# Holding late weight copies behind their step, freeing the gate transposes and moving embedding products in a two-layer decoder trunk

## The chip, the cores and the metric

The kernel runs on one core of a Trainium2 chip. The metric is the device time of one execution in microseconds (us), as a median over runs. A core has a matrix engine (PE, with its weight loads shown as PEld), a vector engine (DVE), a scalar engine (ACT), a general engine (POOL) and a queue engine that issues most of the DMA transfers (SP). Each works through its own list of instructions in order, and they wait for one another through semaphores. The order of each list is fixed when the program is built.

## The reference

The input is x, 512 tokens of 1024 features. Two layers follow one another; each is a mixer, a gated MLP with a causal convolution of width 3, and an input embedding that is gated and added:

```python
for i in range(2):
    h = h + (ab_mixer if i == 0 else nsa_mixer)(rms_norm(h), ...)
    h = h + conv_ffn(rms_norm(h), w_up[i], conv_w[i], conv_b[i], w_down[i])
    e = rms_norm(p[i] @ ple_w[i])                  # 512 x 256 by 256 x 1024
    h = h + sigmoid(rms_norm(h) @ ple_w_gate[i]) * e
```

The change touches the second mixer, `nsa_mixer`, alone. It has 16 query heads of 64 in two groups, and three branches for each head: attention over compressed blocks of keys (`kc`, `vc`), over selected blocks, and over a window. With 512 tokens the selection takes every block and the window covers everything before a query, so both of these are causal attentions over all earlier keys, with keys and values of their own. The three results of a head are weighted by `gates = sigmoid(h @ w_gate + b)`, 48 columns, and summed; then comes an output projection `o @ w_out`.

## The kernel before

All activations lie with features on the 128 partitions, in eight blocks of 128 features by 512 tokens. Products are made in a split form: each operand is cut into a high part (rounded to the fp32r format) and a low part (what is left), and `mm3` (lines 204 to 207) issues three matmuls, high by high, high by low and low by high. A weight of 128 x 1024 is therefore loaded by a DMA on SP into a buffer `wr` (4 of them), copied by ACT into a high part `wh` (3 buffers), and subtracted on DVE or POOL into a low part `wl` (3 buffers). `load_late` (line 169) does this in three separate steps: it issues the DMA, with a raised priority, and gives back two functions, one for the high part on ACT and one for the low part on POOL. Both stand on line 175, which is how the profile names them.

A scheduler orders what the Python code traces. It goes by priority, which is the order of the trace unless a block raises it, and lets an instruction go ahead of earlier ones when its inputs and buffers are there by its own estimate. `self.behind(engine)` limits that: the instructions traced inside it are placed on that engine after the last instruction that had been traced for it up to then.

The mixer begins with projections. `thin()` makes the 48 gate values as rows, `sg` (its last step is the sigmoid on line 823), and `gate_columns(sg)` turns them into columns: four PE transposes (line 829) into a PSUM bank, a DVE copy (line 830) and a small DVE multiplication. These stand among the products of the first query half (`q0`, lines 205 to 207) and of the small network that compresses keys (`hidden_step`, lines 903 to 906). In the kernel before, the call comes after the third `hidden_step` and is held behind it on PE.

The attention itself is a list of 96 steps, six for each head, made by `UNITS`: query blocks 3, 3, 2, 2, 1 and 0, the larger ones with one branch at a time and the smaller ones with both. A step makes scores on PE (lines 1096 and 1097), the masked maximum on DVE (1099), the exponential and its sum on ACT (1101), and the scaling by the gate on POOL (1112). Four steps later (`LAG`) the same unit is transposed on PE (1127), copied as a high part on ACT (1130), given its low part on DVE (1389), and after two more steps multiplied with the values on PE (1152). A head's result is copied out by ACT (1159, 1162), put together by SP's DMAs (1165 to 1168) and added and split on POOL (1182 to 1184).

Between these, other jobs are put into the steps by a planner written in the kernel. `load` holds an estimate in ns for each engine ("T" is PE, "V" DVE, "S" ACT, "G" POOL) and step; `then(step, jobs)` puts a job into the first step from `step` on in which no engine falls behind by more than `SLACK`, at `PACE` = 1950 ns a step; and a job of a step is traced at its end. The jobs that matter here are these.

- `embed(m, s0)`: block m of the embedding product of layer 1, two `mm3` (six matmuls), then a copy out of PSUM on ACT (line 1692; for the first steps on DVE) and a DMA on SP that stores it (line 1693). `EMBED_AT[m]` is its first step. It is called for m below `emb.done` = `KD - LEFT` = 7; the eighth block is made at the start of the MLP instead. `EMBED_AT[4]` is also the step for which the second half of the embedding's weight is loaded.
- `out_first(m, s0)`: half of block m of the output projection, four `mm3`, from step `OUT_AT[m]` = 63, 67, 72, 78, 86, 99, 101, 103 on.
- `late(step, src, use)`: a weight by `load_late`. The DMA is traced eight steps ahead of `step`, the high part from six ahead, the low part a step later. It is used for the embedding's second weight (step 12), four weights of the output projection's first half (for steps 63, 72, 86 and 101) and two of its second half (steps 100 and 102). With the planner's own numbers the six high parts of the output projection's weights fall on steps 57, 66, 80, 95, 96 and 97. In the kernel before, a low part of a weight used after step 40 is held behind POOL's last traced instruction, and a high part is not held.

Of the kernel before, what the change touches and what calls it, by code (L numbers as in the profile page):

```python
# [34 lines left out]
Q1_AT = 0  # L35
LAST_AT = (100, 102)
PACE, SLACK = 1950, {"T": 2500, "V": 1000, "S": 1000, "G": 1500}
EMBED_AT = (0, 1, 2, 6, 12, 17, 22, 27)
OUT_AT = (63, 67, 72, 78, 86, 99, 101, 103)
UNITS = ((3, (0,)), (3, (1,)), (2, (0,)), (2, (1,)), (1, (0, 1)), (0, (0, 1)))  # L40
BANKS = {"a": 4, "b": 3, "o": 1}
# [25 lines left out]
class Trunk:  # L67
# [706 lines left out]
    def nsa_mixer(self):  # L774
        nc, I, tc = self.nc, self.I, self.tc
# [3 lines left out]
        with ExitStack() as ctx:  # L779
# [28 lines left out]
            def thin():  # L808
                self.cycle = ("b",)
                ps = [self.ws(I["w_cmp"][w], n) for w in range(2)]  # L810
                self.norm_scale(n)
                hT = []
                for w in range(2):
                    t = self.sc()
                    nc.vector.tensor_tensor(t, ps[w], n.b, ALU.mult)
                    hT.append(t)
                w, ps = self.packed(I["w_ngate"]), self.ps("o")
                self.cycle = ("a",)
                for k in range(KD):
                    self.packed_step(ps, w, n, k)  # L820
                sg = self.packed_sum(ps)
                nc.vector.tensor_tensor(sg[0:48], sg[0:48], n.b[0:48], ALU.mult)
                nc.scalar.activation(sg[0:48], sg[0:48], AF.Sigmoid, bias=self.col(C_NGB, 0, 48))
                return hT, sg

            def gate_columns(sg):
                pt = self.ps("b")
                for j in range(NTT):
                    nc.tensor.transpose(pt[:, 48 * j : 48 * j + 48], sg[0:48, j * P : (j + 1) * P], self.ident[0:48, 0:48])
                nc.vector.tensor_copy(gate.rearrange("p a b c -> p (a b c)"), pt[:, 0 : 48 * NTT])  # L830
                nc.vector.tensor_scalar(gate[:, 0, :, 0], gate[:, 0, :, 0], valid, None, ALU.mult)
# [64 lines left out]
            def hidden_step(which, xs, ph, c):  # L896
                hi, lo = self.load(I["w1"][which, c])
                for q in range(4):
                    jj = 4 * c + q
                    ws = slice(256 * q, 256 * q + 256)  # L900
                    x = xs[c // 2][:, jj % 8]
                    if jj:
                        nc.tensor.matmul(ph[0:64, 0:256], x[:, 0], lo[:, ws], start=False, stop=False)
                    nc.tensor.matmul(ph[:, 0:256], x.rearrange("p a s -> p (a s)"), hi[:, ws], start=jj == 0, stop=jj == 15)
                    if jj == 0:
                        nc.tensor.matmul(ph[0:64, 0:256], x[:, 0], lo[:, ws], start=False, stop=False)
# [285 lines left out]
            hT, sg = thin()  # L1192
# [9 lines left out]
            xv = blocks(1, hT[1])  # L1202
            q0 = self.Tokens(self, I["w_q"][0], n)
            q0.steps(0, 1)
            hidden_step(0, xk, ph, 2)
            with self.behind(nc.tensor):
                gate_columns(sg)
            q0.steps(1, 2)
            hidden_step(0, xk, ph, 3)
            hk = hidden(ph)  # L1210
# [69 lines left out]
            def fits(e, step, n):  # L1280
                late = 0
                for k in range(step + 12):
                    late = max(0, late + load[e][k] + n * (k == step) - PACE)
                    if k >= step and late > SLACK[e]:
                        return False
                return True

            def then(step, *jobs):
                for e, n, f in jobs:
                    if f is None:  # L1290
                        step += n
                        continue
                    while not fits(e, step, n):
                        step += 1
                    load[e][step] += n
                    todo[step].append(f)
                    step += 1
                return step

            def stack(sts, hd, s0):  # L1300
                got = []
                copy = "VS"[hd % 2 == 0], 620, lambda: q_stack_copy(hd, got[0])
                last = then(s0, ("T", 440, lambda: got.append(q_stack_t(sts, hd, "b" if s0 < LAG else "a"))), copy)
                assert last <= 6 * hd, ("stack", hd, last)
                return last

            def comp_first(c, s0):
                got = {}
                x = lambda name, *a: lambda: getattr(got["x"], name)(*a)
                last = then(s0, ("T", 530, lambda: (got.update(x=Compressed(c, "a")), got["x"].products(0))))  # L1310
                then(last, ("V", 840, x("masked", 0)))
                last = then(last, ("T", 530, x("products", 1)), ("V", 840, x("masked", 1)))
                last = comp_last(got, last, ("V", 680, x("maxima")), ("G", 1050, x("shift")), ("", 1, None))
                assert last <= 24 * c + LAG + VALUES_LAG + 2, (c, last)
# [6 lines left out]
            def late(step, src, use):  # L1321
                got = []

                def low():
                    with self.behind(nc.gpsimd) if step > 40 else ExitStack():
                        got[2]()

                todo[max(step - 8, 0)].append(lambda: got.extend(self.load_late(src)))
                then(max(step - 6, 2), ("S", 1060, lambda: got[1]()), ("G", 1500, low))
                todo[step].append(lambda: use(got[0]))  # L1330

            def embed(m, s0):
                got = []
                then(s0, ("T", 1360, lambda: got.append(emb.products(m, ew[m // 4], "b" if s0 < LAG else "a"))), ("V" if s0 < LAG else "S", 650, lambda: emb.keep(m, got[0], s0 < LAG)))

            def out_first(m, s0):
                got = []
                then(s0, ("T", 2720, lambda: got.append(self.out_products(wo[m // 2], m, *outs[0]))), ("V", 690, lambda: self.out_add(m, got[0])))
# [17 lines left out]
            comp_first(2, max(stack(sts1, 8 + i, ready_at + 1 + i) for i in range(4)))  # L1356
            comp_first(3, max(stack(sts1, 12 + i, 52 + 2 * i) for i in range(4)) + 1)
            late(EMBED_AT[4], I["w_ple"][1, 1], lambda w: ew.append(w))
            for i in range(4):
                late(OUT_AT[2 * i], I["w_nso"][0, i], lambda w, i=i: wo.update({i: w}))  # L1360
            for i in range(2):
                late(LAST_AT[i], I["w_nso"][1, i], lambda w, i=i: wo.update({4 + i: w}))
            for m in range(KD):
                if m < emb.done:
                    embed(m, EMBED_AT[m])
                out_first(m, OUT_AT[m])
# [494 lines left out]
```

## Time and profile before

| | |
|---|---|
| median of 3 runs | 1321.82 us (1321.33 to 1322.67) |
| the profiled execution | 1321.43 us, of which the span from first to last instruction is 1319.7 us |
| PE busy | 1309.3 us, 99% of the span, 7730 matmuls |
| PEld (weight loads) | 1147.9 us, 87% |
| DVE, ACT, POOL busy | 1023.1, 743.4 and 345.9 us (78, 56 and 26%) |
| granted TensorE clock | full |
| the 96 steps of the attention | scores from 729.0 to 879.6 us |

Times within the profile count from the span's start. A row of the timeline has the start, the duration, the engine, the line, the operation, output and inputs by their names in the program, and how many of its kind follow one another; in brackets stands the idle time of the engine before it and what ended it. Matmuls overlap: the next one starts before the modelled end of the one before, so rows of one engine can add up to more than the time between them, and a PE that waits for less than this overlap shows no idle time at all. A row of the windows has the stretch, its length, and for each engine its busy time and its number of instructions.

### The profile page before, as it was taken

The page shows a single profiled execution, that of the slowest core. Times are in us where ns is not written, and L with a number is a line of the kernel's source. Part 1 is how long each engine was busy: PE and PEld are TensorE (multiplying, and loading weights), DVE is VectorE, ACT ScalarE, POOL GpSimd, SP SyncE. Part 2 cuts the span into 40 slices and gives each one's busy share as a digit, 9 for nine tenths or more (in the row PEclk, how much of TensorE's full clock was granted, in tenths as well). Part 3 has the DMA queues.
Part 4 walks back from the last instruction along what each step waited for, and adds up shares of the span by engine and source line. Part 5 has one row for each costly group of instructions (what it writes and reads, how often), then busy time and mean ns, then how long its engine had stood idle before and what let it go on. Part 6 is the DMA issues. An engine that isn't in the chain of part 4 may idle for free.

```text
span 1319.7 us, 21157 instructions
## 1 busy us (share of the span) xinstructions
PE 1309.3 (99%) x7730; PEld 1147.9 (87%) x7730; DVE 1023.1 (78%) x1842; ACT 743.4 (56%) x1315; POOL 345.9 (26%) x380
## 2 busy tenths in 40 slices
PE   9999999999999999999999999999999999999998
PEld 7888887889999999988788889888889999999887
DVE  6866887697888877678778888867798887877676
ACT  5357535555555555345466889775365555555342
POOL 3356420011111110330230867771011111100320
PEclk9999999999999999999999999999999999999999
DMA  6532335665666553334243211114666666643421
GB/s 244 158 107 83 125 97 164 190 181 152 177 176 170 152 133 95 129 101 134 85 159 118 75 37 54 49 37 132 187 172 167 181 172 170 162 124 93 132 96 64
DMA packets 72480, 172.75 MB, mean 131 GB/s; under 512 B 8500, under 2 KB 15284, under 8 KB 72376
## 3 DMA queue, kind: packets, MB, share of 16 engines
q1 hardware_dynamic: 62584, 153.96, 36.6%
q0 software_dynamic: 9504, 17.31, 8.0%
q8 instruction: 61, 1.00, 0.3%
q14 instruction: 43, 0.35, 0.1%
q10 hardware_dynamic: 288, 0.14, 0.0%
HBM read 149.34 MB, written 7.35 MB: 119 GB/s over the span
## 4 chain that ended last, share of the span: by engine, by line
PE 95%; DVE 4%; ACT 1%; issue 1%; DMA 0%; POOL 0%; ACTq 0%; DVEq 0%
PE ps L205 27%; PE ps L206 27%; PE ps L207 27%; PE ps L1152 3%; PE ps L1127 2%; PE ps L1096 1%; PE ps L1097 1%; PE ps L484 1%; DVE wl L146 1%; PE ps L339 1%; PE ps L1022 1%; ACT wh L145 1%; PE ps L1045 1%; PE ps L353 0%; DVE xf L890 0%
## 5 line engine op out<-in xcount | busy, mean ns | idle before, releaser
L145 ACT ACTIVATE wh<-wr 128x1024 fp32r<-128x1024 f32 (+2 forms) x181 | 185.9, 1029 | 226.0 <-PE ps L206 159.1
L206 PE MATMUL ps<-y,wh 128*128 128x512 f32 (+1 forms) x754 | 263.3, 350 | 0.0
L205 PE MATMUL ps<-y,wh 128*128 128x512 f32 (+1 forms) x754 | 262.9, 354 | 0.2
L207 PE MATMUL ps<-y,wl 128*128 128x512 f32 (+1 forms) x754 | 261.7, 350 | 0.0
L146 DVE TENSOR_TENSOR wl<-wr,wh 128x1024 fp32r<-128x1024 f32 (+2 forms) x164 | 200.1, 1222 | 53.1 <-ACT wh L145 51.9
L205 PEld LDWEIGHTS ps<-y,wh 128*128 128x128 f32 x754 | 142.5, 189 | 21.4 <-DVE sc L1722 0.9
L207 PEld LDWEIGHTS ps<-y,wl 128*128 128x128 f32 x754 | 142.6, 189 | 19.2 <-DVE wl L146 0.4
L206 PEld LDWEIGHTS ps<-y,wh 128*128 128x128 f32 x754 | 142.7, 189 | 18.8
L205 PE MATMUL ps<-g,wh 128*128 128x512 f32 x384 | 150.0, 391 | 0.0
L206 PE MATMUL ps<-g,wh 128*128 128x512 f32 x384 | 149.8, 390 | 0.0
L207 PE MATMUL ps<-g,wl 128*128 128x512 f32 x384 | 149.4, 389 | 0.0
L1530 POOL DMA_DIRECT2D ep<-ep x33 | 28.6, 867 | 347.3 <-DMA ep<-in_w_up_dram 79.7
L1537 POOL DMA_DIRECT2D es<-in_w_up_dram x33 | 28.9, 889 | 220.0 <-DVE sc L1500 139.0
L1606 DVE TENSOR_TENSOR hp<-hp,ps 128x512 f32<-128x512 f32 x96 | 65.5, 682 | 27.0 <-PE ps L207 27.0
L207 PEld LDWEIGHTS ps<-g,wl 128*128 128x128 f32 x384 | 72.1, 188 | 15.3
L205 PEld LDWEIGHTS ps<-g,wh 128*128 128x128 f32 x384 | 72.2, 188 | 14.1
L206 PEld LDWEIGHTS ps<-g,wh 128*128 128x128 f32 x384 | 72.2, 188 | 13.6
L1112 POOL TENSOR_SCALAR pr<-pr,sm,gate 128x512 f32<-128x512 f32 (+3 forms) x128 | 76.3, 609 | 28.3 <-DVE sm L1110 22.4
L1573 ACT ACTIVATE sc<-ps 128x256 f32<-128x256 f32 x132 | 50.1, 380 | 59.6 <-PE ps L207 57.7
L1101 ACT ACTIVATE pr<-pr,nmx 128x512 f32<-128x512 f32 (+3 forms) x128 | 71.4, 564 | 6.9 <-DVE nmx L1099 5.5
L205 PE MATMUL ps<-y,gh 128*128 128x256 f32 x264 | 74.9, 284 | 0.0
L207 PE MATMUL ps<-y,gl 128*128 128x256 f32 x264 | 74.7, 283 | 0.0
(383 smaller groups left out, 3326.1 us busy)
## 6 DMA issues: line engine op xcount, KB each, us to landing
wr<-in_w_up_dram SPq DMA_DIRECT2D x55, 512.0 KB, 3.6
ep<-in_w_up_dram SPq DMA_DIRECT2D x33, 512.0 KB, 5.8
wr<-in_w_down_dram SPq DMA_DIRECT2D x64, 256.0 KB, 3.0
es<-in_w_up_dram SPq DMA_DIRECT2D x33, 256.0 KB, 2.8
ep<-ep POOLq DMA_DIRECT2D x33, 256.0 KB, 3.5
es<-in_w_up_dram POOLq DMA_DIRECT2D x33, 256.0 KB, 6.4
wr<-in_w_plg_dram SPq DMA_DIRECT2D x16, 512.0 KB, 3.5
wr<-in_w_down_dram SPq DMA_DIRECT2D x32, 192.0 KB, 2.8
```

Source lines behind the costliest of these rows:

```text
L145: self.nc.scalar.activation(hi, src, AF.Copy)
L146: (eng or self.nc.vector).tensor_tensor(lo, src, hi.bitcast(F32), ALU.subtract)
L205: mm(out, ah, bh, start=first, stop=False, **kw)
L206: mm(out, ah, bl, start=False, stop=False, **kw)
L207: mm(out, al, bh, start=False, stop=last, **kw)
L1101: nc.scalar.activation(pr[:, b], pr[:, b], AF.Exp, scale=-1.0, bias=nmx[:, b : b + 1], accum_out=sm[:, bs[b] : bs[b] + 1])
L1112: nc.gpsimd.tensor_scalar(prs[b], prs[b], sm[:, b : b + 1], gate[:, j, hd, 1 + b : 2 + b], ALU.mult, ALU.mult)
L1152: nc.tensor.matmul(po[0:m, cols], vv[i][:, b, g, 0:m], src, start=False, stop=last and b == 1 and i == 0 and part == 0)
L1530: nc.gpsimd.dma_start(me.two[:, :T], me.two[:, T:], accum_op=ALU.add)
L1537: nc.gpsimd.dma_start(me.s3, I["w_up"][i, me.f][:, :T], accum_op=ALU.add)
L1573: copy = lambda out, ps: nc.scalar.activation(out, ps, AF.Copy)
L1606: nc.vector.tensor_tensor(self.h[m], self.h[m], ps, ALU.subtract)
```

## The change

Three edits, all within the second mixer.

```diff
-EMBED_AT = (0, 1, 2, 6, 12, 17, 22, 27)
+EMBED_AT = (0, 1, 2, 6, 12, 22, 32, 41)
...
             q0.steps(0, 1)
+            gate_columns(sg)
             hidden_step(0, xk, ph, 2)
-            with self.behind(nc.tensor):
-                gate_columns(sg)
             q0.steps(1, 2)
...
                 got = []
 
-                def low():
-                    with self.behind(nc.gpsimd) if step > 40 else ExitStack():
-                        got[2]()
+                def held(x, eng):
+                    with self.behind(eng) if step > 40 else ExitStack():
+                        got[x]()
 
                 todo[max(step - 8, 0)].append(lambda: got.extend(self.load_late(src)))
-                then(max(step - 6, 2), ("S", 1060, lambda: got[1]()), ("G", 1500, low))
+                then(max(step - 6, 2), ("S", 1060, lambda: held(1, nc.scalar)), ("G", 1500, lambda: held(2, nc.gpsimd)))
```

The last three entries of `EMBED_AT` are later by 5, 10 and 14 steps. `gate_columns` is called ahead of the third `hidden_step` instead of after it, and may be placed anywhere from there. The high part of a late weight used after step 40 is now also held, behind the last instruction traced for ACT in the step where the planner puts it.

## The prediction

> **What bounds the kernel now.** I read the page's busy times first, then the chain that ended last.
>
> ```profile
> span 1319.7 us, 21157 instructions
> PE 1309.3 (99%) x7730; PEld 1147.9 (87%) x7730; DVE 1023.1 (78%) x1842; ACT 743.4 (56%) x1315; POOL 345.9 (26%) x380
> ...
> PE 95%; DVE 4%; ACT 1%; issue 1%; DMA 0%; POOL 0%; ACTq 0%; DVEq 0%
> ```
>
> PE is idle for 1319.7 - 1309.3 = 10.4 us of the whole span, and the chain is PE's for 95% of it. No edit takes work from PE, so all that this change can win is idle time of PE within its reach, and all that it can lose is new idle time. Where the idle time lies, the windows of the second mixer show (stretch, length, then busy time and instructions of PE, PEld, DVE, ACT and POOL):
>
> ```profile
> 645.00:662.00 17.00, 16.10 (x74) 13.02 (x73) 14.26 (x19) 8.02 (x12) 7.17 (x9) 1.00 0.25 83
> 662.00:705.00 43.00, 42.22 (x231) 35.27 (x230) 33.49 (x87) 28.52 (x53) 10.40 (x12) 1.00 0.43 139
> ...
> 741.00:753.00 12.00, 11.99 (x89) 10.82 (x87) 9.81 (x35) 12.00 (x37) 12.00 (x18) 1.00 0.29 100
> 753.00:765.00 12.00, 12.00 (x88) 10.74 (x89) 11.58 (x40) 11.26 (x33) 9.21 (x15) 1.00 0.17 46
> 765.00:777.00 12.00, 12.00 (x92) 11.06 (x91) 8.79 (x30) 10.39 (x26) 7.10 (x11) 1.00 0.11 33
> ...
> 783.00:786.00 3.00, 2.34 (x18) 1.91 (x18) 3.00 (x13) 3.00 (x10) 0.86 (x2) 1.00 0.41 87
> 786.00:789.00 3.00, 2.09 (x20) 1.91 (x17) 1.91 (x11) 2.17 (x11) 2.95 (x4) 1.00 0.00 0
> ```
>
> PE lacks 0.90 us in the first row, 0.78 in the second, and 0.66 + 0.91 = 1.57 in the last two: 3.25 us, 0.25% of the time. That is the ceiling of any gain, but for pauses too short to show. Around the attention's steps 8 to 16 (741 to 753) ACT is busy for all 12.00 us, and at 783 to 786 both ACT and DVE are busy for all 3.00 while PE waits. The view of PE's waits names the first two gaps, the timeline the last two:
>
> ```profile
> PE ps L206 <- DVE wl L146: 0.9, 1, 0.9
> PE ps L205 <- ACT wh L145: 0.8, 1, 0.8
> ```
>
> ```profile
> 784.98 0.92 PE L1152 MATMUL ps<-pt,vv 128*64 128x256 f32 x6 [0.66 <-DVE pt L1389]
> ...
> 788.19 0.66 PE L1127 MATMUL ps<-ident,pr 128*128 128x128 f32 x4 [0.91 <-POOL pr L1112]
> ```
>
> The first two are weight splits of the projections. The other two are the attention's own chain: DVE's low parts of probabilities, and POOL's scaling.
>
> **The embedding products.** `EMBED_AT` changes in three places, but `embed` is called for m below 7, so the last entry (27 to 41) is never read. Two products move, m = 5 and m = 6. The load of their weight hangs on entry 4, which stays at step 12. In the timeline of PE they stand here, and the scores give the scale of steps:
>
> ```profile
> 755.39 0.45 PE L205 MATMUL ps<-wh,wh 128*128 128x512 f32 x1
> ...
> 756.81 0.39 PE L1096 MATMUL ps<-hp,y 128*128 128x512 f32 x1
> ...
> 765.17 0.48 PE L205 MATMUL ps<-wh,wh 128*128 128x512 f32 x1
> ```
>
> ```profile
> L1096 PE MATMUL ps<-hp,y x48: 278/392/496, 729.0 to 800.8; 128*128 128x512 f32 x24, 128*128 128x384 f32 x16, 128*128 128x256 f32 x8
> ...
> L1096 PE MATMUL ps<-ep,y x48: 280/401/481, 801.8 to 879.6; 128*128 128x512 f32 x24, 128*128 128x384 f32 x16, 128*128 128x256 f32 x8
> ```
>
> A product takes 756.81 - 755.39 = 1.42 us of PE. m = 5 goes to where m = 6 stands now, about 765, and m = 6 to step 32, about 729.0 + 32 x (800.8 - 729.0) / 47 = 778. So from 755 to 778 PE is 1.42 us ahead of where it was, if the other engines keep up, and then has 1.42 us of work that waits for nobody a few us before the gaps at 784 and 788. Each product also moves an ACT copy (0.58 us, below) and an SP store. If ACT and DVE do not keep up, PE merely pauses earlier by what it would have waited later, and the gain is nothing; if they do, it is the smaller of 1.42 and 1.57.
>
> **The high parts.** The planner places the six copies on steps 57, 66, 80, 95, 96 and 97. The scheduler ran them far ahead of that, as the rows on ACT show (the first of seven belongs to the embedding's weight):
>
> ```profile
> L175 ACT ACTIVATE wh<-wr x7: 1043/1061/1066, 728.7 to 883.6; 128x1024 fp32r<-128x1024 f32 x7
> ```
>
> ```profile
> 739.45 1.04 ACT L175 ACTIVATE wh<-wr 128x1024 fp32r<-128x1024 f32 x1
> ```
>
> ```profile
> 767.13 1.05 ACT L175 ACTIVATE wh<-wr 128x1024 fp32r<-128x1024 f32 x1
> 768.08 0.58 ACT L1692 ACTIVATE y<-ps 128x512 f32<-128x512 f32 x1
> 768.55 1.06 ACT L175 ACTIVATE wh<-wr 128x1024 fp32r<-128x1024 f32 x1
> ```
>
> Three of them, 3.15 us, lie in the stretch in which ACT is fullest, one at 739 ahead of the 12.00 of 12.00, two at 767 to 770. With them and the copy of m = 5 gone, ACT has 1.04 + 0.58 = 1.62 us less to do before 765 and 2.11 less right after it. That is why I think ACT can follow PE's 1.42 us. DVE loses nothing, but has 12.00 - 8.79 = 3.21 us idle from 765 to 777. Of the range 0 to -1.57 for both edits I take -1.2, nearer the full end; the second gap hangs on POOL's queue too, so not all of it:
>
> ```profile
> 786.05 1.33 POOL L1182 TENSOR_TENSOR sc<-sc,sc 128x512 f32<-128x512 f32 x1 [2.19 <-PE ps L1127]
> 787.36 1.52 POOL L1112 TENSOR_SCALAR pr<-pr,sm,gate 128x512 f32<-128x512 f32 x2
> ```
>
> The scaling at 787.36, for which PE waits, stands behind an addition of head results that held POOL until 786.05.
>
> What the copies cost where they go: behind ACT's last instruction of the step queue later copies (line 1130) and exponentials, and for those wait DVE, POOL and PE. Step 57 is about 801.8 + 9 x (879.6 - 801.8) / 47 = 817, step 66 about 832.
>
> ```profile
> 816.00:819.00 3.00, 3.00 (x26) 2.76 (x25) 2.62 (x9) 3.00 (x9) 1.50 (x3) 1.00 0.10 22
> ...
> 822.00:825.00 3.00, 3.00 (x29) 2.96 (x29) 1.77 (x7) 2.02 (x7) 3.00 (x4) 1.00 0.00 0
> ...
> 828.00:831.00 3.00, 3.00 (x18) 2.51 (x18) 2.10 (x6) 0.61 (x3) 3.00 (x5) 1.00 0.34 109
> ...
> 852.00:855.00 3.00, 3.00 (x24) 2.70 (x23) 1.42 (x7) 0.75 (x5) 2.19 (x4) 1.00 0.00 0
> ```
>
> At 817 ACT has no room (3.00 of 3.00) and gets some only at 822 to 825 (0.98 idle), so 1.05 us of delay can reach PE, which has no output product yet (the first is allowed at step 63): 0 to +1.05, of which I take +0.2, since PE is without a pause there and hence ahead of ACT's results. Near 832 ACT has just idled 2.39 us, and the output products cover: 0, or 1.05 without that cover. Step 80 is about 855, after 2.25 us of idle ACT in three: 0 as well.
>
> The last three move to the tail, behind the exponentials of step 95:
>
> ```profile
> 886.82 0.39 ACT L1101 ACTIVATE pr<-pr,nmx 128x128 f32<-128x128 f32 x1
> ```
>
> ```profile
> 883.99 0.44 PE L205 MATMUL ps<-y,wh 128*128 128x512 f32 x1
> ...
> 884.74 0.39 PE L206 MATMUL ps<-y,wh 128*128 128x512 f32 x1
> ...
> 887.80 0.45 PE L205 MATMUL ps<-y,wh 128*128 128x512 f32 x1
> ```
>
> ```profile
> 888.51 7.55 POOL L175 TENSOR_TENSOR wl<-wr,wh 128x1024 fp32r<-128x1024 f32 x3
> ```
>
> At 883.99 and 887.80 PE runs parts of an output product that need only a high part, before its low part starts at 888.51. With the high part made after 887 the group from 883.99 to 884.74 (two matmuls with the high part for each of two blocks, about 0.9 us) cannot run there, and the other one perhaps not: 0 to +1.8 us. The work is not lost, only its use as filler is, and the low parts start no later than now as long as one copy of 1.06 us after 887.2 is through by about 888.5. I take +0.3.
>
> **The gate transposes.**
>
> ```profile
> L829 PE MATMUL ps<-ident,sc x4: 223/240/262, 671.4 to 673.3; 48*128 48x48 f32 x4
> ```
>
> ```profile
> 658.54 0.72 ACT L823 ACTIVATE sc<-sc,cols 48x512 f32<-48x512 f32 x1
> ```
>
> Their input is ready at 659.26; PE is then in the gap that waits for `wl` (0.9 us). If they land there, four at up to 0.24 us fill at most 0.9 of idle time; if they land later, it is 0; if PE's list has them ahead of matmuls that are ready before 659.26, they could cost about 0.5. From -0.9 to +0.5 I take -0.1, since the list is in no way tied to that gap.
>
> **The sum.** -1.2 + 0.2 + 0.3 - 0.1 = -0.8 us. The span becomes 1318.9; with the 1321.43 - 1319.7 = 1.73 us around it 1320.6 for the profiled execution, and as the median lies 0.39 above that one, 1321.0 us.
>
> The Trainium skill (Perfetto Trace Analysis, "Identifying the Most-Contended Engine") warns that matmul busy time is a poor measure and that the weight loads' share is a good one. By that share (87%) PE would have some 170 us of room, and the sum above would be no ceiling. The trace disagrees here: from 753 to 765 PE has not a pause, its six matmuls at 755 follow one another every 1.42 / 6 = 0.24 us, and yet the weight loads fill only 10.74 of 12.00 us. A share below 100% is thus what a full PE looks like in this kernel, and I keep the ceiling.
>
> **The rivals.**
>
> 1. *All gaps go* (faster). ACT's relief carries through, the transposes fill the gap at 659, and the reordering closes the one at 703 too: -3.25 us at most, 1318.6. For it: 3.15 us of ACT leave the fullest stretch. Against it: the gap at 703 is touched by no edit. For over 0.2% it takes 2.64 of the 3.25. Chance 0.20.
> 2. *The gap only moves* (no change). DVE's 3.00 of 3.00 at 783 to 786 is the real bound; PE, relieved at 755, waits at 760 instead: 1321.8, or 1322.3 with the two small costs. For it: DVE is at 11.58 of 12.00 from 753 to 765. Chance 0.22.
> 3. *The tail opens* (slower). The three copies, 3 x 1.06 = 3.2 us, stand on ACT one after the other ahead of the last units' copies of probabilities, and PE has lost its filler: with the gain away, 1321.8 + 3.2 = 1325.0. It decides once all three stand ahead of the copy that PE needs and the output products still wait for low parts. Against it stands that ACT has room there, 1.15 us of every 3.00 from 889 on:
>
> ```profile
> 889.00:892.00 3.00, 3.00 (x27) 2.73 (x25) 1.68 (x4) 1.85 (x4) 3.00 (x2) 1.00 0.20 42
> ```
>
>    Chance 0.08.
> 4. *SP's list* (slower). An SP store waits for its ACT copy, and SP's later transfers behind it:
>
> ```profile
> 768.69 0.33 SPq L1693 DMA_DIRECT2D emb<-y  x1
> ...
> 782.93 0.46 SPq L1167 DMA_DIRECT2D sc<-sc  x1
> ```
>
>    The store of m = 6 now falls next to the head's copies at 782.93, which POOL's addition at 786.05 needs. Each us that it holds them is one for PE; with 3 us, 1324.8. Chance 0.05.
>
> The forecast with its own range (1319.5 to 1322.5) has the rest, 0.45.
>
> **How the numbers follow.** About 0.2%, 2.6 us, can be told from no change here. Faster than 1319.2 is rival 1: 0.20. Slower than 1324.5 are rivals 3 and 4: 0.13. The rest, 0.67, is no measurable change. The range must take in most of rival 1, whose floor is 1318.6, and the unknown costs (+1.05, +1.8 and +0.5 without any gain would give 1325.2, but all at once is unlikely): 1318.3 to 1323.9.
>
> **What would show it.** Right: scores of steps 18 to 22 start about 1.4 us earlier, no L175 on ACT between 730 and 800, PE full from 783 to 789, a `wh,wh` product near 778. Wrong: a new idle time of PE before 778 (rival 2), between 816 and 825, or from 884 to 895 (rival 3), or POOL held longer by line 1182 (rival 4). A gain of over 3.3 us would mean that pauses too short to show in these views count, or that the order changed elsewhere.

## The result, and the profile after

The changed kernel takes 1330.22 us (median of 6 runs, 1328.47 to 1331.45) against 1321.82 us before. The ratio is 1.0062, with a 95% interval of 1.0052 to 1.0073: it is slower by 8.4 us, where 1321.0 was forecast. The profiled execution took 1328.97 us, 7.54 more than the one of before. In the kernel after, the lines behind the gate's transposes have numbers lower by one: line 1389 of before, the low parts of the probabilities, is now line 1388. The head of the page:

```profile
span 1327.3 us, 21150 instructions
...
PE 1311.5 (99%) x7730; PEld 1149.2 (87%) x7730; DVE 1028.4 (77%) x1842; ACT 743.5 (56%) x1315; POOL 344.9 (26%) x380
```

PE's work is the same 7730 matmuls, yet it is idle for 15.8 us (10.4 before) and busy for 2.2 us longer. Windows over the second mixer show where. First before, then after; the columns are stretch, length, then busy time and instructions of PE, PEld, DVE, ACT and POOL, then granted clock, DMA share and GB/s:

```profile
640.00:728.00 88.00, 86.31 (x454) 71.92 (x453) 67.49 (x147) 51.18 (x90) 22.66 (x25) 1.00 0.41 132
...
753.00:780.00 27.00, 27.00 (x199) 24.53 (x200) 23.38 (x81) 24.30 (x67) 18.03 (x26) 1.00 0.13 36
780.00:792.00 12.00, 10.41 (x77) 9.10 (x76) 9.95 (x39) 10.34 (x31) 9.22 (x14) 1.00 0.16 35
792.00:885.00 93.00, 93.00 (x655) 83.67 (x654) 76.62 (x268) 79.05 (x229) 70.26 (x98) 1.00 0.18 49
885.00:898.00 13.00, 13.00 (x93) 11.65 (x92) 6.21 (x14) 4.54 (x12) 12.26 (x11) 1.00 0.36 107
```

```profile
640.00:728.00 88.00, 86.69 (x458) 72.67 (x457) 68.18 (x148) 52.10 (x92) 22.43 (x26) 1.00 0.41 132
...
753.00:780.00 27.00, 24.94 (x186) 22.30 (x185) 22.42 (x80) 20.66 (x60) 16.52 (x24) 1.00 0.10 26
780.00:792.00 12.00, 12.00 (x89) 10.97 (x89) 10.67 (x39) 11.55 (x36) 10.67 (x16) 1.00 0.17 46
792.00:885.00 93.00, 92.39 (x651) 82.55 (x650) 76.26 (x267) 78.80 (x229) 70.08 (x97) 1.00 0.20 51
885.00:898.00 13.00, 8.32 (x64) 7.44 (x63) 10.24 (x13) 7.07 (x15) 11.54 (x11) 0.92 0.32 96
```

PE's idle time changes by -0.38 us in the first stretch, +2.06, -1.59 and +0.61 in the attention, and +4.68 in the tail. The last one also drags the clock down. The waits of PE name the two large losses:

```profile
PE ps L1152 <- DVE pt L1388: 4.9, 2, 4.7
PE ps L1127 <- POOL pr L1112: 1.8, 1, 1.8
```

**The tail.** The timeline of PE, of DVE and of POOL there:

```profile
892.54 0.39 PE L206 MATMUL ps<-y,wh 128*128 128x512 f32 x1
897.61 1.54 PE L1152 MATMUL ps<-pt,vv 128*64 128x256 f32 x6 [4.68 <-DVE pt L1388]
```

```profile
889.35 1.16 DVE L1388 TENSOR_TENSOR pt<-ps,pt 128x512 fp32r<-128x512 f32 x2 [0.32 <-ACT pt L1130]
891.06 6.02 DVE L1178 TENSOR_TENSOR sc<-sc,sc 64x512 f32<-64x512 f32 x1 [0.56 <-DMA sc<-sc]
897.02 1.47 DVE L1388 TENSOR_TENSOR pt<-ps,pt 128x384 fp32r<-128x384 f32 x3
```

```profile
889.50 7.05 POOL L175 TENSOR_TENSOR wl<-wr,wh 128x1024 fp32r<-128x1024 f32 x3
```

PE idles until the three low parts that DVE makes from 897.02 on. DVE has them in line behind line 1178, an addition of half a tile, which at the end of DVE's list costs PE nothing (below). That addition took 6.02 us, and it ended half a us after the last of POOL's three subtractions. In the kernel before it stood behind all but one of the low parts, and took 1.27 us:

```profile
892.53 1.27 DVE L1178 TENSOR_TENSOR sc<-sc,sc 64x512 f32<-64x512 f32 x1 [0.28 <-DMA sc<-sc]
...
895.58 0.69 DVE L402 TENSOR_TENSOR hp<-hp,ps 128x512 f32<-128x512 f32 x1 [1.46 <-PE ps L207]
```

The order of DVE's list around it, before and after (tile numbers shortened):

```
before: L1389 low part, L1389 low part, L1389 low part, L1178 addition, L1389 low part
after:  L1388 low part, L1178 addition, L1388 low part, L1388 low part, L1388 low part
```

**The clock.** Windows of after behind the pause, with the granted clock as the third number from the end:

```profile
895.00:898.00 3.00, 0.39 (x2) 0.39 (x3) 3.00 (x3) 0.00 (x0) 1.54 (x1) 0.64 0.65 194
898.00:901.00 3.00, 3.00 (x11) 2.60 (x11) 0.48 (x2) 0.00 (x0) 0.00 (x0) 0.50 0.43 156
901.00:904.00 3.00, 3.00 (x11) 2.36 (x10) 0.69 (x1) 0.00 (x0) 0.00 (x0) 0.72 0.00 0
```

A granted clock of 0.50 means about half the work: matmuls of 512 columns follow one another every 0.42 us at 899 and every 0.23 us at 892. With PE busy again from 897.61, 3.00 x 0.50 + 3.00 x 0.28 + about 0.2 of the first row are some 2.5 us lost, an estimate from these rows. The pause of 4.68 us thus costs about 7.2. With the changes of idle time above (-0.38 + 2.06 - 1.59 + 0.61 + 4.68 = 5.4) the sum is 7.9, against 7.54 measured. The Trainium skill (TensorE: Matmul & The Clock Gate, "What's actually happening") has the clock go to one half after an idle window of about 3.4 us; this trace agrees for the pause of 4.68 us. Pauses of 2.1 and 2.2 us, shorter than such a window, were followed by a half clock as well (below), and there the measurement differs.

**The middle.** The timeline of SP's queue, POOL and PE of after, near 765:

```profile
760.41 0.47 SPq L1167 DMA_DIRECT2D sc<-sc  x1
760.94 0.59 SPq L1168 DMA_DIRECT2D sc<-sc  x1
```

```profile
760.49 0.89 POOL L1112 TENSOR_SCALAR pr<-pr,sm,gate 128x128 f32<-128x128 f32 x2 [1.07 <-PE ps L1127]
764.69 1.27 POOL L1182 TENSOR_TENSOR sc<-sc,sc 128x512 f32<-128x512 f32 x1 [3.31 <-DMA sc<-sc]
765.93 1.53 POOL L1112 TENSOR_SCALAR pr<-pr,sm,gate 128x512 f32<-128x512 f32 x2
```

```profile
766.76 0.66 PE L1127 MATMUL ps<-ident,pr 128*128 128x128 f32 x4 [1.81 <-POOL pr L1112]
```

It is the same pattern on another engine. An addition whose inputs travel by two DMAs (issued at 760.41 and 760.94; the row names a DMA as what ended the wait, at 764.69) stands in POOL's list ahead of the two scalings for which PE waits, and POOL idles for 3.31 us in front of it.

### The profile page after: what moved, and what is told of

Its sections match the earlier page's. It is cut to its first block, busy times and chain, and to the rows that moved or that the text cites. A ratio compares the mean times of both kernels' runs of the same rounds, so it can differ in the third digit from the quotient of the medians.

```text
span 1327.3 us, 21150 instructions
## 1 busy us (share of the span) xinstructions
PE 1311.5 (99%) x7730; PEld 1149.2 (87%) x7730; DVE 1028.4 (77%) x1842; ACT 743.5 (56%) x1315; POOL 344.9 (26%) x380
## 4 chain that ended last, share of the span: by engine, by line
PE 94%; DVE 3%; ACT 2%; issue 1%; DMA 0%; POOL 0%; ACTq 0%; DVEq 0%; POOLq 0%
PE ps L205 27%; PE ps L207 27%; PE ps L206 27%; PE ps L1152 3%; PE ps L1127 2%; PE ps L1096 1%; PE ps L1097 1%; PE ps L484 1%; DVE wl L146 1%; PE ps L339 1%; PE ps L1045 1%; PE ps L353 0%; ACT wh L145 0%; DVE xf L890 0%; DVE sc L1178 0%
```

## The experiments

Each is compared with the kernel before in the same batch of runs. In kernels with added lines the numbers shift: line 1178 is line 1177 where it is held back, line 1182 is 1181 or 1186, and the low parts of line 1389 are on lines up to 1396.

**Which part does it.** First the changed kernel with its high parts free again, then the kernel before with the high parts held and nothing else.

```
-  ("S", 1060, lambda: held(1, nc.scalar))
+  ("S", 1060, lambda: got[1]())
```

> The changed kernel without the hold on high parts (gate transposes and embedding products moved as in the change). Theory A, order: the hold reordered DVE's list in the tail, so that the addition of the last heads (line 1178) stands ahead of three low parts that PE needs and cannot finish while POOL subtracts; without the hold the loss goes: 1320 to 1322 us, no PE wait over 1 us after 880. Theory B, ACT: the held copies delay ACT and take PE's filler; also 1320 to 1322. Theory C, the moved products: the loss comes from these and stays, 1329 us or more.

> The kernel before with only the hold on high parts. Theories A and B: all of the loss, 1328 to 1331 us, with PE waiting 4 to 5 us near 892 and a half clock after it. Theory C: 1321 to 1323 us.

Without holding: 1321.93 us, ratio 1.0002 [0.9993, 1.0011], no loss. Holding alone: 1326.07 us, ratio 1.0036 [1.0023, 1.0049], a loss, but a smaller one than the 1328 to 1331 expected. Line 1178 again:

```profile
888.14 5.98 DVE L1178 TENSOR_TENSOR sc<-sc,sc 64x512 f32<-64x512 f32 x1 [0.55 <-DMA sc<-sc]
```

So holding brings the pause of the tail. That pause lies 3 us earlier here than in the changed kernel (888.14 against 891.06): holding wins time ahead of it, which the other parts lose.

**The addition's place.** In the changed kernel line 1178 is held behind all that DVE has been given; or the three high copies of the tail alone are freed.

```
+  def sum_low():
+      with self.behind(nc.vector):
+          nc.vector.tensor_tensor(one[0:64], one[0:64], two[0:64], ALU.add)
...
-  lambda: nc.vector.tensor_tensor(one[0:64], one[0:64], two[0:64], ALU.add),
+  sum_low,
```

> The changed kernel with one instruction moved: the addition of line 1178 is placed on DVE behind its last traced instruction, as it needs nothing but transfers it had been let ahead. All holds stay. Theory A: the PE wait near 892 shrinks from 4.7 us to under 1 us, the clock stays full, 1320 to 1323 us. Theory B: the held copies still delay ACT, so most of the loss stays, 1327 us or more. Theory C: 1329 us.

```
-  lambda: held(1, nc.scalar)
+  lambda: held(1, nc.scalar) if step < 100 else got[1]()
```

> The changed kernel with the hold kept for the three high parts of steps 57, 66 and 80 and taken from the three of steps 95 to 97. Theories A and B: 1320 to 1322 us, since the place is the tail. Theory C: 1329 us. If the holds in the middle cost what the prediction allowed (up to 1 us near 817), it shows against the run without any hold.

1324.0 us (1.0014 [1.0004, 1.0023]) and 1323.82 us (1.0014 [1.0005, 1.0024]). The pause of the tail is gone in both, but both times lie above what was expected. With the tail's copies free, DVE's list again has the addition behind three of the low parts: it is the three held copies that moved it, though no run shows by which of the scheduler's estimates. What remains is the pause at 765, 2.1 and 2.2 us long. Both kernels' runs fall into two groups, near 1321.8 and near 1324. The mean granted clock of a run is 0.998 in the upper group, with one run at 0.999, and 0.999 or 1.000 in the lower. The profiled executions are of the upper group, and show half a clock behind that pause too, here with the addition late:

```profile
768.00:771.00 3.00, 3.00 (x18) 2.94 (x19) 1.25 (x2) 1.21 (x3) 3.00 (x5) 0.60 0.00 0
771.00:774.00 3.00, 3.00 (x18) 2.69 (x17) 1.09 (x5) 1.77 (x3) 2.79 (x4) 0.83 0.21 44
```

**The other parts alone, and holding with the addition late** (the kernel before with `EMBED_AT` of the change; with the gate's transposes in their new place; with the high parts held and `sum_low` as above).

> The kernel before with the two embedding products moved, and nothing else. Theory M (the pause of PE at 764 to 767 comes from the product of 755 that is missing there, whatever else is changed): PE waits for POOL's scaling there by 1.5 to 2.3 us, and the time is 1321.5 to 1324, no gain. Theory N (that pause needs the held high copies too, which let PE run further ahead of POOL): no wait above 1.0 us at 764 to 767, the gaps at 784 and 788 shrink, 1320.5 to 1321.5. In both line 1178 takes about 1.3 us as before and there is no tail pause, since no high copy of the tail is held.

> The kernel before with the gate's transposes not held, and nothing else. My step in the prediction: -0.1 us (between -0.9 and +0.5), so 1321.0 to 1322.3, with PE's wait near 658 shorter by about 0.4 to 0.6 us (the profile of after shows 0.38 us more PE time in the stretch 645 to 662) and nothing different after 700.

> The high parts held as in the change, products and gate as before, and the addition of line 1178 held behind everything DVE has been given. Theory A (the loss of holding alone is only the place of that addition on DVE, ahead of three low parts and beside POOL's subtractions): no pause of PE above 1 us in the tail, no granted clock below 0.9 after 890, and the 3 us that holding wins ahead of the tail stay: 1317.5 to 1319.5. Theory B (held copies on ACT come too late for the output products and the last units' copies): PE still pauses 2 us or more between 885 and 897, 1323 to 1326.

The moved products alone: 1322.52 us, 1.0007 [0.9998, 1.0016], no gain. Their timeline has PE's pauses at 764 and 768 in place of those of 784 and 788:

```profile
764.59 0.92 PE L1152 MATMUL ps<-pt,vv 128*64 128x256 f32 x6 [0.57 <-DVE pt L1389]
...
768.62 0.55 PE L1074 MATMUL ps<-ident,sc 128*128 128x128 f32 x3 [0.33 <-POOL sc L1069]
```

The waits go by theory N (0.6 us and shorter), the time by theory M (no gain): the gap only moved, and the long pause needs holding too. The gate alone: 1320.96 us, 0.9994 [0.9985, 1.0003]; its trace has 0.38 us less idle time of PE before 728, and the time cannot be told from no change. Holding with the addition late: 1319.29 us, 0.9981 [0.9972, 0.9990]. Theory A is borne out: the late copies on ACT cost PE nothing that shows, and the gaps of 784 and 788 are all but closed:

```profile
780.00:792.00 12.00, 11.93 (x88) 10.47 (x87) 10.93 (x42) 11.77 (x37) 11.04 (x18) 1.00 0.11 24
...
885.00:898.00 13.00, 13.00 (x80) 11.21 (x79) 5.72 (x10) 6.57 (x12) 8.92 (x6) 1.00 0.41 131
```

**Is it POOL?** Holding alone, with the addition ahead of three low parts, but the tail's weights split by DVE.

```
-  lambda: self.nc.gpsimd.tensor_tensor(lo, raw, hi.bitcast(F32), ALU.subtract)
+  lambda: (eng or self.nc.gpsimd).tensor_tensor(lo, raw, hi.bitcast(F32), ALU.subtract)
...
+  eng = nc.vector if step >= 100 else nc.gpsimd
```

> Holding alone, but the low parts of the tail's three weights are made by DVE and not by POOL; the addition of line 1178 stays ahead of three low parts of probabilities in DVE's order, as in the run that holds alone. Theory A1 (the addition is blocked by POOL's subtractions): it takes 0.6 to 0.9 us, and PE has no pause of 4 us; DVE has three subtractions of about 1.2 us more, so pauses of PE up to 1.5 us may remain; 1317.5 to 1320.5. Theory A2 (its place in the order or its late DMA makes it slow, POOL is a bystander): it still takes 4 us or more and the time stays near 1326.

1319.48 us, 0.9982 [0.9973, 0.9991]. The addition still leads the low parts, and takes 0.68 us:

```profile
888.86 0.68 DVE L1178 TENSOR_TENSOR sc<-sc,sc 64x512 f32<-64x512 f32 x1
```

So it was POOL's subtractions that held the addition. Does it get a turn between two of them? In the kernel that holds alone, each of the three is now cut into eight instructions:

```
+  for c in range(pieces):
+      s = slice(1024 // pieces * c, 1024 // pieces * (c + 1))
+      self.nc.gpsimd.tensor_tensor(lo[:, s], raw[:, s], hi[:, s].bitcast(F32), ALU.subtract)
```

> Holding alone, with each of the tail's three low parts on POOL cut into eight subtractions of 128x128. DVE's order is unchanged: line 1178 ahead of three low parts of probabilities. Theory B1 (DVE's addition gets its turn at a boundary between two POOL instructions): it takes at most 0.7 + 0.4 = 1.1 us or little more, PE has no pause above 1.5 us in the tail, and the time is 1318.5 to 1320.5. Theory B2 (it gets its turn only when POOL has nothing to run): it takes 5 us or more, and the time stays at 1325.5 to 1328.

1327.86 us, 1.0049 [1.0032, 1.0065]. Line 1178 is line 1184 here. DVE, then POOL:

```profile
888.49 9.01 DVE L1184 TENSOR_TENSOR sc<-sc,sc 64x512 f32<-64x512 f32 x1 [0.56 <-DMA sc<-sc]
```

```profile
886.92 10.04 POOL L179 TENSOR_TENSOR wl<-wr,wh 128x128 fp32r<-128x128 f32 x24
```

The addition began during the fourth piece, let twenty boundaries pass, and ended at 897.50, 0.54 us after POOL's last piece (896.96). Theory B2 holds here. In the kernel before, however, the addition did get a turn, between the second subtraction and the third (892.53 to 893.80), and the third then took 2.85 us instead of 2.38 or 2.40:

```profile
L175 POOL TENSOR_TENSOR wl<-wr,wh x3: 2377/2400/2849, 888.5 to 893.2; 128x1024 fp32r<-128x1024 f32 x3
```

The same happened in the four other kernels in which the tail's high copies are free (without holding; with the tail's copies alone free; the products alone; the gate alone): the addition began during the second of three subtractions, took 0.82 to 1.30 us, and the third took 2.85 to 2.87. In the kernels in which it stood still it had begun during the first, or the fourth of 24. What decides this is open; no run varies it alone.

**The middle.** Four kernels, all with the high parts held and line 1178 late: without the moved products; with all of the change, and also POOL's additions of head pairs held behind what POOL has been given; without the gate's part; and with the second product alone moved.

```
-  EMBED_AT = (0, 1, 2, 6, 12, 22, 32, 41)
+  EMBED_AT = (0, 1, 2, 6, 12, 17, 22, 27)
```

> The changed kernel without its moved products: high parts held, gate transposes back, line 1178 held behind DVE's list. If the parts add up (holding with the late addition 1319.29, the gate's transposes alone 0.71 below the kernel before, since 1321.67 - 1320.96), 1318.6, with no pause of PE above 1 us after 730. If the gate's part was only spread between runs, 1319.3.

```
+  def sum_pair():
+      with self.behind(nc.gpsimd):
+          nc.gpsimd.tensor_tensor(one, one, two, ALU.add)
...
-  lambda: nc.gpsimd.tensor_tensor(one, one, two, ALU.add),
+  sum_pair,
```

> The whole change, line 1178 late, and POOL's additions of pairs of heads (line 1182) held behind what POOL has been given. Theory Q (PE's pause of 2.2 us at 765 comes from one such addition that stands in POOL's order ahead of the two scalings PE needs, and waits 3.3 us for the heads' transfer): no wait of PE for scaling above 1 us near 765, no clock below 0.9 there, runs no longer in two groups, 1318.0 to 1320.5. Theory R (the missing product at 755 makes PE catch up with DVE and ACT, whatever POOL's order is): a pause of 1.5 us or more stays near 765, only with another releaser, and the time stays at 1321.6 to 1324.

> The changed kernel without its gate part and with line 1178 late: high parts held and products moved. POOL's list again has the addition of a pair of heads ahead of the two scalings. Theory Q and theory R alike: PE waits about 2.2 us for scaling near 765, and the time is 1321.7 to 1324.5, as in the run of the whole change with the addition late. If it is below 1320, the pause needs the gate's part.

```
-  EMBED_AT = (0, 1, 2, 6, 12, 22, 32, 41)
+  EMBED_AT = (0, 1, 2, 6, 12, 17, 32, 41)
```

> The kernel with high parts held, gate transposes back and line 1178 late, in which only the second product moves, from step 22 to 32; the first stays at step 17. POOL's list has both scalings behind line 1069 and the addition, as without any move. Theory P (the filler at 755 is what is needed, that of 765 is free to fill a later gap): no pause above 1 us near 765, 1318.0 to 1318.8, at or just below the kernel without moved products. Theory R (any product taken from 755 to 770 costs a pause there): a pause of 1 us or more near 767, 1319.5 to 1321.5.

Without moved products: 1318.45 us, 0.9974 [0.9965, 0.9984], as the sum of the parts had it (1318.6): the fastest of all, and faster than both kernels. With the pair additions late: 1321.05 us, 0.9994 [0.9985, 1.0004]. The 2-us pause at 765 is gone, as theory Q has it, and with it the second group of runs (1320.37 to 1321.64). But the forecast time did not come, since a pause opened further on, for DVE's low parts:

```profile
786.35 0.92 PE L1152 MATMUL ps<-pt,vv 128*64 128x256 f32 x6 [1.45 <-DVE pt L1396]
```

Without the gate's part: 1324.35 us, 1.0021 [1.0012, 1.0030], with the pause at 765, as both theories had it. With one product moved: 1319.39 us, 0.9981 [0.9972, 0.9989]. Nothing pauses at 767, against theory R, yet it is no better than with none moved, against theory P: the same pattern comes at 803. POOL, then PE:

```profile
803.84 1.27 POOL L1186 TENSOR_TENSOR sc<-sc,sc 128x512 f32<-128x512 f32 x1 [4.37 <-DVE nmx L1099]
```

```profile
805.81 0.55 PE L1127 MATMUL ps<-ident,pr 128*128 128x128 f32 x3 [1.93 <-POOL pr L1112]
```

The heads' copies had been issued from 798.09 on there, between other loads. That POOL waited for their landing is argued: the releaser that the row names, DVE's maximum, is inferred.

## Why the prediction was wrong

**The tail, +0.3 (bounds 0 to +1.8).** This term failed. Holding alone against holding with the addition late measured 1326.07 - 1319.29 = 6.8 us (two batches, whose kernels before lie 0.1 us apart). The term asked what PE lacks as filler and whether ACT is through in time. ACT was, nearly: its copies for the three low parts that PE missed were done at 891.02 and 892.74, and PE ran until 892.93. ACT's timeline of after:

```profile
890.52 0.50 ACT L1130 ACTIVATE pt<-ps 128x384 fp32r<-128x384 f32 x1
890.89 1.08 ACT L175 ACTIVATE wh<-wr 128x1024 fp32r<-128x1024 f32 x1
891.85 0.89 ACT L1130 ACTIVATE pt<-ps 128x512 fp32r<-128x512 f32 x2
```

Nothing asked what the held copies do to the order of DVE's list. Line 1178 was in no step of the prediction, though the trace of before shows it at 1.27 us, next to 0.69 for line 402 with twice the partitions: a DVE instruction that took twice as long while POOL ran, and so a row to ask about. The rule that speaks against the change was to be had: the Trainium skill (SBUF — State Buffer, "🔬 SBUF: two separate sides") gives a DVE instruction with two SBUF inputs and a GpSimd instruction one pair of ports, held by the first for its whole instruction, if POOL's instruction reads SBUF. The traces agree that the addition can be shut out entirely; they differ in how long, 6.02 and 9.01 us over several instructions of POOL, not one.

**The middle, -1.2 for products and high parts together.** The two are opposite. Holding, with its tail mended, wins 1321.67 - 1319.29 = 2.4 us, more than the whole term. The products take it back: 1318.45 us without them, 1324.0 with them (the median of two groups, from another batch), all else the same. The step that failed is that relief of ACT lets PE keep its 1.42 us. PE did get ahead: in the changed kernel the scores numbered 18 to 22 in order of time start 2.5 to 4.1 us earlier than before (1.0 of it from the first score on), but number 23 starts 2.75 us later. The pause at 765 is shown to come from the place of POOL's addition. With that addition late PE waits for DVE at 786 instead, and the time is still 2.6 us above the kernel without the moved products. DVE is busy for 12.00 of 12.00 us from 753 to 765 in the changed kernel; that this fullness is the deeper cause is argued, not shown. Rival 2's row (DVE at 11.58 of 12.00) said so, and for the products alone rival 2 is what happened.

**The copies that move off the fullest stretch** cost what was said or less (terms +0.2, 0 and 0). They run at 817, 837 and 864 in the changed kernel. PE has 3.00 of 3.00 from 816 to 819 there, and 93.00 of 93.00 from 792 to 885 in the kernel that holds with the addition late; the one visible pause of the changed kernel in that stretch, 0.47 us at 809, lies ahead of the first held copy. **The gate**, -0.1: its transposes did land in the gap, at 659.3, and the gap is 0.38 us shorter, inside the bounds of -0.9 to +0.5. (The view gives 0.26 us as the longest of the four transposes; the 0.24 of the prediction is the median.)

**The rivals.** Rival 3 had the place and the sign, but its mechanism, ACT's copies one after the other for 3.2 us, is not what happened: the price was about 7.2 us, by DVE behind POOL and a halved clock. The clock was no term of any rival, since before has 1.00 in every row I quoted. Rival 4 had line 1182 holding POOL, but at 765 and not by SP's list: the transfer was issued at 760.41, 0.02 us after its ACT copy ended. Rival 1's 1318.6 is reached by the parts without the products and with line 1178 late (1318.45). Its profiled execution is 2.5 us below that of before (1318.94 against 1321.43); 1.9 of them are idle time of PE (10.4 against 8.5) and 0.6 its busy time, which may hide pauses shorter than the overlap of two matmuls; no view shows them.

**The signs.** No copy of line 175 ran on ACT between 730 and 800, PE was full from 783 to 789, and a product ran at 780: these came as said. The earlier scores came too, by more than the 1.4 us expected. New idle time before 778 and from 884 to 895, and POOL waiting at line 1182, were the signs named for being wrong.

## What to carry to other kernels

A change of when instructions may start also changes their order in every engine's list, so look in the trace of before for instructions that wait for a DMA just beside the critical ones: one place further forward, they made the whole engine wait, for the transfer on POOL and behind another engine on DVE. An instruction that takes longer than others of its size beside another engine's work, as line 1178 did in the trace of before, is a sign of the second kind. Filler taken from a full stretch came back as a pause, there or some tens of us further on, though the engine freed of it had room. And PE's pauses of 2 us and more could have a second price, the clock.

## What the runs showed that was not expected

- A DVE addition with two SBUF inputs stood still for as long as POOL's subtractions followed each other: 6.02 us beside instructions of 2.4 us, 9.01 beside pieces of 0.47, and 0.68 without POOL. Low parts of probabilities, which read PSUM and SBUF, ran beside POOL without such a delay (1.16 us for two at 889.35, against 1.15 where DVE splits the weights).
- Pauses of PE of 2.1 and 2.2 us were followed by a half clock in the profiled executions, and the times of these kernels fall into two groups 2 us apart. That the faster executions had no half clock there is argued from their mean clocks, as none of them was profiled; the changed kernel, after its 1.81 us at 765, had a granted clock of 1.00.
- From the rows above, as an estimate, the half clock lasted 2 x 3.00 x (0.40 + 0.17) = 3.4 us after the pause of 2.1 us, and 2 x 3.00 x (0.36 + 0.50 + 0.28) = 6.8 us after that of 4.68, in part while PE still paused.
